# Mamba-2 chunk outputs: mask and log of dt inside the exponential, one product with C B for both directions

## The chip, the cores and the metric

One Trainium2 chip; the kernel runs on one of its cores. The metric is the device time of one execution in microseconds. The profile shows the core's engines: TensorE (PE, its weight loads apart as PEld), VectorE (DVE), ScalarE (ACT), GpSimd (POOL), and the queues that start DMA transfers (SP above all).

## The reference, cut to what matters

One layer of a hybrid trunk over 256 context and 1024 latent tokens, 1024 wide: a projection, three token mixers side by side (a Mamba-2 SSD, a gated unit, an S5 scan), a projection back and an MLP of 4096. The change lies in the SSD, which runs in both directions over chunks of 128 tokens, with 8 heads of 64 in two groups that share B and C. For one direction:

```python
a_cum = jnp.cumsum(dt * a.reshape(SSD_GROUPS, R), axis=2)
xdt = x * dt[..., None]
seg = a_cum[:, :, :, None] - a_cum[:, :, None, :]
lower = jnp.tril(jnp.ones((CHUNK, CHUNK), dtype=bool))[:, :, None, None]
lmat = jnp.exp(jnp.where(lower, seg, -jnp.inf))
cb = jnp.einsum('bcqgn,bckgn->bcqkg', cm, bm)
y_diag = jnp.einsum('bcqkg,bcqkgr,bckgrp->bcqgrp', cb, lmat, xdt)
...
y_off = jnp.einsum('bcqgn,bcgrpn,bcqgr->bcqgrp', cm, h_prev, jnp.exp(a_cum))
y = (y_diag + y_off).reshape(b_, L, H, P)
```

The mixer adds both directions and a skip term (`ssd_d` times x); `h_prev` is the state carried from chunk to chunk.

## The kernel before

There are 1280 tokens in 10 chunks (2 context, 8 latent) and two head groups g, so 20 chunks of outputs. `dt_chain` (L734 to L778) computes dt once for all chunks and both directions (`DTD`), the cumulative sums along the partitions (`col`: that of the forward direction, and the negative of the backward one), the factors for the states (`wdec`, `dtot`), and the same sums as rows, which it stores to DRAM (`rows_d`, L778).

`ssd_group` (L829) has two generators for a group. `right` (L869) runs the backward states over the chunks and keeps each as `hb`. `outputs` (L883) makes the outputs of one chunk a step:

- It loads the chunk's x, B and C (`xc`) and, by a DMA that gives every partition the same rows, `rb`: 2 directions x 4 heads x 128 sums (512 KB, three buffers).
- ScalarE takes exponentials of rb for the states' part (`er`, two halves of the partitions, L897).
- For each head ScalarE adds a column of `col` to rb's second half (L900) and VectorE subtracts the other column from the first half and takes the minimum (L901), which is the right one of the two differences on either side of the diagonal; one exponential over the four heads follows (L902).
- TensorE transposes x and B (`tok_major`, L842) and multiplies B by C into PSUM (`pcb`, L904). VectorE masks that product with the two triangles of `tri` into `cm` (L906).
- For each head ScalarE multiplies one triangle by dt (L910), and VectorE multiplies the other by its dt and adds (L911); VectorE multiplies all four heads by the exponentials (L912).
- TensorE multiplies the result by x into `py` (L918, eight parts of 64 rows in the trace) and the states by C into `po` (L925). VectorE scales `po` by er (L927), adds the skip term (L929, into cm again), GpSimd adds the two directions of er (L931), VectorE adds that (L932), and cm is stored (L933).
- `new_state` (L850) carries the forward state on: VectorE makes `xw`, TensorE multiplies it by B (L854), GpSimd decays the old state (L860), VectorE adds.

Each group's steps are handed to a scheduler together with other work: the slabs of the input projection whose columns these chunks need or that come behind (`xbc_slab`, `z_slab`), the S5 mixer's gate (`s5_glu`), `mixed_tile` and the first output projections (`out_slab`). The scheduler (`schedule_with_timeline_sim=True`, L1611) decides the order of the instructions on every engine. Helpers record most operations: L54 (`tt`, two tensors), L57 (`stt`, a tensor with a scalar column and a second tensor), L60 (`act`), L48 (`load`), so in the profile these are told apart by their tiles.

The tile that a chunk's masks and outputs share, and the order in which rb is used, in code:

```python
cm = pool.tile([128, 2, 128], F32, tag="cm", name="cm", bufs=2)
tt(cm, pcb.unsqueeze(1).to_broadcast([128, 2, 128]), tri[:, 0:2], ALU.mult)
...
    act(rb[:, 0, hh], cm[:, 0], ACT.Copy, scale=d0[:, hh:hh + 1])
    stt(rb[:, 0, hh], cm[:, 1], d1[:, hh:hh + 1], rb[:, 0, hh], ALU.mult, ALU.add)
tt(rb[:, 1], rb[:, 1], rb[:, 0], ALU.mult)
```

Of the kernel before, what the change touches and what calls it, by code (L numbers as in the profile page):

```python
# [10 lines left out]
F32 = mybir.dt.float32  # L11
F32R = mybir.dt.float32r
ACT = mybir.ActivationFunctionType
ALU = mybir.AluOpType
# [28 lines left out]
def trunk_kernel(ctx: ExitStack, tc: tile.TileContext, I, O):  # L43
# [690 lines left out]
    def dt_chain():  # L734
# [30 lines left out]
        for i, (m, d) in enumerate(((0, 0), (1, 1), (2, 0), (3, 1))):  # L765
            T.matmul(pc[:, i * 80:(i + 1) * 80], lhsT=tri[:, m, :], rhs=dta[:, d, :], start=True, stop=True)
        T.matmul(pc[:, 320:480], lhsT=ones, rhs=dta.rearrange("p d c -> p (d c)"), start=True, stop=True)
        S.copy(col[:, 0], pc[:, 0:80])
        act(col[:, 1], pc[:, 80:160], ACT.Copy, scale=-1.0)
        act(wdec.rearrange("p d c -> p (d c)"), pc[:, 160:320], ACT.Exp)  # L770
        tt(wdec, wdec, DTD, ALU.mult)
        act(dtot.rearrange("p d c -> p (d c)"), pc[:, 320:480], ACT.Exp)
# [53 lines left out]

    def ssd_group(pool, g):  # L829

        hb = {1: None}

# [35 lines left out]

        def right():  # L869
            px, bt, _ = tok_major(chunk_xbc(1, 3))  # L870
            hb[0] = new_state(f"hb{g}", 9, 1, 1, px, bt, None, "hb")
            yield
            px, bt, _ = tok_major(chunk_xbc(0, 3))
            hbf = new_state("hf", 2, 1, 0, px, bt, hb[0], "hbf")
            load(O["ssdo"][:, 512 + g * 256:512 + (g + 1) * 256], hbf)
            hb[9] = init(1, f"hb{g}", 9)
            yield
            for c in range(9, 2, -1):
                px, bt, _ = tok_major(chunk_xbc(c, 3))
                hb[c - 1] = new_state(f"hb{g}", 9, 1, c, px, bt, hb[c], "hb")  # L880
                yield

        def outputs():  # L883
            hf = None
            for c in range(NCH):
# [1 line left out]
                    load(O["ssdo"][:, g * 256:(g + 1) * 256], hf)  # L887
                    hf = init(0, "hf", 2)
                xc = chunk_xbc(c, 4)
                rb = pool.tile([128, 2, 4, 128], F32, tag="rb", name="rb", bufs=3)  # L890
                load(rb, rows_d[:, c * 8 + g * 4:c * 8 + g * 4 + 4, :].partition_broadcast(128))
                cf, cbk = scal(col, 0, c), scal(col, 1, c)

                er = pool.tile([128, 2, 2, 128], F32, tag="er", name="er", bufs=3)
                for par in range(2):
                    rs = slice(par * 64, (par + 1) * 64)
                    act(er[rs], rb[rs].rearrange("p d (a e) q -> p d a e q", e=2)[:, :, :, par], ACT.Exp)  # L897

                for hh in range(4):
                    act(rb[:, 1, hh], rb[:, 1, hh], ACT.Identity, bias=cbk[:, hh:hh + 1])  # L900
                    stt(rb[:, 1, hh], rb[:, 0, hh], cf[:, hh:hh + 1], rb[:, 1, hh], ALU.subtract, ALU.min)  # L901
                act(rb[:, 1], rb[:, 1], ACT.Exp)  # L902
                px, bt, pcb = tok_major(xc)
                T.matmul(pcb, lhsT=xc[:, 2], rhs=xc[:, 3], start=True, stop=True)  # L904
                cm = pool.tile([128, 2, 128], F32, tag="cm", name="cm", bufs=2)
                tt(cm, pcb.unsqueeze(1).to_broadcast([128, 2, 128]), tri[:, 0:2], ALU.mult)  # L906

                d0, d1 = scal(DTD, 0, c), scal(DTD, 1, c)
                for hh in range(4):
                    act(rb[:, 0, hh], cm[:, 0], ACT.Copy, scale=d0[:, hh:hh + 1])  # L910
                    stt(rb[:, 0, hh], cm[:, 1], d1[:, hh:hh + 1], rb[:, 0, hh], ALU.mult, ALU.add)  # L911
                tt(rb[:, 1], rb[:, 1], rb[:, 0], ALU.mult)  # L912
                xs = pool.tile([128, 4, 64], F32, tag="xs", name="xs", bufs=2)
                S.copy(xs, px)
                py = bank("wb", 2)[:, 0:256].rearrange("p (a q) -> p a q", a=2)
                for a in range(2):
                    for par in range(2):
                        T.matmul(py[par * 64:(par + 1) * 64, a, :], lhsT=xs[:, 2 * a + par], rhs=rb[:, 1, 2 * a + par],  # L918
                                 start=True, stop=True)
                hs_ = (hf, hb[c])  # L920
                dirs = [d for d in range(2) if hs_[d] is not None]
# [3 lines left out]
                        T.matmul(po[:, d, a], lhsT=hs_[d][:, a * 128:(a + 1) * 128], rhs=xc[:, 3], start=True, stop=True)  # L925
                ds = slice(dirs[0], dirs[-1] + 1)
                tt(er[:, ds], po[:, ds], er[:, ds], ALU.mult)  # L927
                for a in range(2):
                    stt(cm[:, a], xc[:, a], dcol[:, 2 * g + a:2 * g + a + 1], py[:, a], ALU.mult, ALU.add)  # L929
                if len(dirs) == 2:  # L930
# [143 lines left out]
    dt_chain()  # L1074
    psA.close()
    with tc.tile_pool(name="pd", bufs=1) as pd, banks("psB"):
        (right0, out0), (right1, out1) = [ssd_group(pd, g) for g in range(2)]
        def drain(g):
            for _ in g:
                pass  # L1080

        drain(right0)
        for m in (2, 3, 5, 7):
            xbc_slab(m)
        for c, _ in enumerate(out0):
            if c >= 5:
                next(right1, None)
                next(right1, None)
        drain(right1)
        for m in (0, 1):  # L1090
            z_slab(m, z_weights(m), (0, 1, 2))
        s5_glu()
        for c, _ in enumerate(out1):
            if c == 0:
                wz = [z_weights(m) for m in (2, 3)]
            if c in (0, 4):
                for m in (2, 3):
                    z_slab(m, wz[m - 2], (2,) if c else (0, 1))
            if c == 7:
                acc = [acc_tile(m) for m in range(4)]  # L1100
                wo = [out_weights(m) for m in range(2)]
                for m in range(2):
                    out_slab(m, (0,), wo[m])
            if c in (2, 6):
                mixed_tile(c // 4)
        stt(gs2, mod[:, 32:40, :], 1.0, g2.unsqueeze(2).to_broadcast([128, 8, 2]), ALU.add, ALU.mult)
        for m in range(2):
            out_slab(m, (1,), wo[m])
        for m in (2, 3):
            out_slab(m, (0, 1))  # L1110
# [504 lines left out]
```

## Time and profile before

| | |
|---|---|
| median of 3 runs | 1580.24 us (1580.15 to 1582.12) |
| the profiled execution's own time | 1578.67 us |
| its span, first to last instruction | 1576.7 us |
| TensorE busy | 1423.4 us (90%) |
| VectorE busy | 1067.9 us (68%) |
| ScalarE busy | 751.1 us (48%) |
| GpSimd busy | 389.5 us (25%) |
| mean granted TensorE clock | 0.947 of full speed |

Shares over the whole span mix stages: the output chunks fill some 200 us of it, the MLP most of the rest. What a change in one stage can do is read from that stage's windows and waits. A row of the lines view gives a group's line, engine, operation and tiles (out<-in), shapes and count, then its busy time in us, the mean of one in ns, and the engine's idle time just before with what ended it. In the timeline a row begins with the start and the duration in us; an xN at its end counts instructions merged into it.

### The profile page before, as it was taken

Reading aid. Unit: us, or ns where it says so; the run is one execution under the profiler, and the core shown is the slowest. Engines: PE = TensorE matmul, PEld = TensorE weight load, DVE = VectorE, ACT = ScalarE, POOL = GpSimd, SP = SyncE. Lnnn points to the kernel's source line nnn. Section 1 sums busy time; section 2 is a strip of 40 time slices with the busy share of each in tenths; the row PEclk is TensorE's granted clock in tenths of the full one; section 3 lists DMA queues with packets and bytes.
Section 4 is the critical chain, followed back from the end, with each engine's and each line's share of the span. In section 5 each row is a group of like instructions: output and inputs, shape, how many; then the busy total and the mean of one; then the engine's idle time right before and its main releaser. Section 6 shows DMA issues by size and latency. Waiting matters only on the chain.

```text
span 1576.7 us, 23817 instructions
## 1 busy us (share of the span) xinstructions
PE 1423.4 (90%) x8360; PEld 1202.6 (76%) x8360; DVE 1067.9 (68%) x1929; ACT 751.1 (48%) x1541; POOL 389.5 (25%) x487
## 2 busy tenths in 40 slices
PE   4689898999787779989999999999899999999795
PEld 3567676778565568878888888888788888887795
DVE  5773368668667885558977764674564768979945
ACT  3643434456645753437655554554555334424322
POOL 4555466613011122321100000000241313032033
PEclk9699999999997879999999999999999999999897
DMA  9759785264675647346444443344744245315312
GB/s 326 251 174 252 227 285 159 88 171 119 181 228 149 172 145 236 122 123 195 138 158 149 149 139 116 125 148 151 250 149 146 70 158 174 121 54 182 112 35 100
DMA packets 238903, 253.29 MB, mean 161 GB/s; under 512 B 15648, under 2 KB 163136, under 8 KB 238784
## 3 DMA queue, kind: packets, MB, share of 16 engines
q1 hardware_dynamic: 222880, 234.51, 48.2%
q10 hardware_dynamic: 15904, 17.27, 3.4%
q8 instruction: 66, 1.08, 0.3%
q14 instruction: 53, 0.43, 0.1%
HBM read 182.82 MB, written 68.89 MB: 160 GB/s over the span
## 4 chain that ended last, share of the span: by engine, by line
PE 58%; DVE 8%; DMA 6%; ACT 2%; issue 2%; POOL 1%; SPq 0%; DVEq 0%; ACTq 0%; POOLq 0%
PE ps_w L1215 7%; PE ps_w L1213 7%; PE ps_w L1214 7%; PE ps_w L1369 6%; PE ps_w L1370 6%; PE ps_w L1371 6%; PE ps_mm L219 4%; PE ps_mm L221 4%; PE ps_mm L220 4%; DMA rb<-rows_d 2%; PE ps_mm L1371 1%; PE ps_mm L1370 1%; PE ps_mm L1369 1%; DVE X L54 1%; DVE rb L57 1%
## 5 line engine op out<-in xcount | busy, mean ns | idle before, releaser
L219 PE MATMUL ps_mm<-hi,wh 128*128 128x512 f32 (+1 forms) x576 | 211.6, 367 | 20.1 <-DVE dtr L707 16.0
L221 PE MATMUL ps_mm<-hi,wl 128*128 128x512 f32 (+1 forms) x576 | 209.4, 364 | 0.9 <-DVE wl L54 0.9
L220 PE MATMUL ps_mm<-lo,wh 128*128 128x512 f32 (+1 forms) x576 | 209.8, 364 | 0.0
L1369 PE MATMUL ps_w<-uB,uA 128*128 128x512 f32 (+1 forms) x520 | 190.6, 371 | 9.3 <-ACT uB L60 8.9
L1370 PE MATMUL ps_w<-uB,uA 128*128 128x512 f32 (+1 forms) x520 | 191.3, 368 | 7.9 <-DVE uB L54 7.9
L1371 PE MATMUL ps_w<-uB,uA 128*128 128x512 f32 (+1 forms) x520 | 190.2, 367 | 0.0
L54 POOL TENSOR_TENSOR cb<-h 128x512 f32<-128x512 f32 x14 | 21.9, 1571 | 512.7 <-DMA h<-w 402.4
L219 PEld LDWEIGHTS ps_mm<-hi,wh 128*128 128x128 f32 x576 | 111.2, 193 | 38.1 <-DVE dtr L707 16.8
L221 PEld LDWEIGHTS ps_mm<-hi,wl 128*128 128x128 f32 x576 | 111.0, 193 | 18.1 <-DVE wl L54 1.8
L220 PEld LDWEIGHTS ps_mm<-lo,wh 128*128 128x128 f32 x576 | 111.0, 193 | 15.0 <-issue 0.6
L1369 PEld LDWEIGHTS ps_w<-uB,uA 128*128 128x128 f32 x520 | 99.9, 193 | 25.2 <-ACT uB L60 9.3
L1370 PEld LDWEIGHTS ps_w<-uB,uA 128*128 128x128 f32 x520 | 100.2, 193 | 24.7 <-DVE uB L54 9.8
L1371 PEld LDWEIGHTS ps_w<-uB,uA 128*128 128x128 f32 x520 | 99.8, 192 | 15.5
L60 ACT ACTIVATE uB<-tb 128x512 fp32r<-128x512 f32 x106 | 65.9, 625 | 64.9 <-PE ps_w L1371 31.7
L54 DVE TENSOR_TENSOR uB<-tb,uB 128x512 fp32r<-128x512 f32 x106 | 87.6, 846 | 13.1 <-ACT uB L60 13.1
L54 DVE TENSOR_TENSOR X<-X,ps_w 128x512 f32<-128x512 f32 x84 | 56.1, 680 | 27.7 <-PE ps_w L1371 27.6
L54 DVE TENSOR_TENSOR q<-q,ps_w 128x512 f32<-128x512 f32 x48 | 32.9, 685 | 59.7 <-PE ps_w L1215 59.0
L54 DVE TENSOR_TENSOR wl<-wraw,wh 128x1024 fp32r<-128x1024 f32 x32 | 48.4, 1514 | 36.7 <-ACT wh L60 35.9
L60 ACT ACTIVATE c<-c 128x512 f32<-128x512 f32 x64 | 40.3, 629 | 57.8 <-DVE c L54 56.9
L1371 PE MATMUL ps_mm<-ch,uA 128*128 128x256 f32 x224 | 63.2, 283 | 0.0
L1370 PE MATMUL ps_mm<-cl,uA 128*128 128x256 f32 x224 | 63.2, 283 | 0.0
L1369 PE MATMUL ps_mm<-ch,uA 128*128 128x256 f32 x224 | 63.1, 283 | 0.0
(435 smaller groups left out, 3875.3 us busy)
## 6 DMA issues: line engine op xcount, KB each, us to landing
rw<-w SPq DMA_DIRECT2D x112, 256.0 KB
tb<-a_d SPq DMA_DIRECT2D x106, 256.0 KB
aw<-ada_w SPq DMA_DIRECT2D x64, 256.0 KB
h<-w SPq DMA_DIRECT2D x32, 512.0 KB
a_d<-t SPq DMA_DIRECT2D x42, 256.0 KB
rb<-rows_d SPq DMA_DIRECT2D x20, 512.0 KB
adaw<-ada_w SPq DMA_DIRECT2D x32, 256.0 KB
wraw<-w_out SPq DMA_DIRECT2D x16, 512.0 KB
```

The source lines that it names most:

```text
L54: eng.tensor_tensor(out=out, in0=a, in1=b, op=op)
L57: V.scalar_tensor_tensor(out=out, in0=a, scalar=sc, in1=b, op0=op0, op1=op1)
L60: S.activation(out=out, in_=in_, func=func, **kw)
L219: T.matmul(out, lhsT=wh(k), rhs=xh(k), start=(k == 0), stop=False)
L220: T.matmul(out, lhsT=wh(k), rhs=xl(k), start=False, stop=False)
L221: T.matmul(out, lhsT=wl(k), rhs=xh(k), start=False, stop=(k == nk - 1))
L1213: T.matmul(out, lhsT=wh, rhs=X[0][:, j, :], start=(j == 0), stop=False)
L1214: T.matmul(out, lhsT=wh, rhs=X[1][:, j, :], start=False, stop=False)
L1215: T.matmul(out, lhsT=wl, rhs=X[0][:, j, :], start=False, stop=(j == 3))
L1369: T.matmul(out, lhsT=wh, rhs=bh, start=start, stop=False)
L1370: T.matmul(out, lhsT=wh, rhs=bl, start=False, stop=False)
L1371: T.matmul(out, lhsT=wl, rhs=bh, start=False, stop=stop)
```

## The change

`dt_chain` now fills `col` with log(dt) minus the cumulative sum, for both directions, with dt held above 1e-37. A constant tile `cap` is 0 where a direction's triangle holds and -1e30 elsewhere. In `outputs` GpSimd adds cap to each direction's rows into a tile of its own, `sg` (two buffers); ScalarE takes eight exponentials, one for each direction and head, with the column of col as bias, so that mask and dt are inside the exponential; VectorE adds the two directions and multiplies the sum by C B straight from PSUM. rb has two buffers in place of three, the output cm has a tile of its own with three, and the two groups share 16 buffers of backward states.

```diff
--- before.py
+++ after.py
@@ dt_chain
-        S.copy(col[:, 0], pc[:, 0:80])
-        act(col[:, 1], pc[:, 80:160], ACT.Copy, scale=-1.0)
+        V.tensor_scalar(out=col, in0=DTD, scalar1=1e-37, scalar2=None, op0=ALU.max)
+        act(col, col, ACT.Ln)
+        fl = col.rearrange("p d c -> p (d c)")
+        tt(fl, fl, pc[:, 0:160], ALU.subtract)
...
@@ ssd_group
-            hb[0] = new_state(f"hb{g}", 9, 1, 1, px, bt, None, "hb")
+            hb[0] = new_state("hb", 16, 1, 1, px, bt, None, "hb")
...
-                rb = pool.tile([128, 2, 4, 128], F32, tag="rb", name="rb", bufs=3)
+                rb = pool.tile([128, 2, 4, 128], F32, tag="rb", name="rb", bufs=2)
                 load(rb, rows_d[:, c * 8 + g * 4:c * 8 + g * 4 + 4, :].partition_broadcast(128))
-                cf, cbk = scal(col, 0, c), scal(col, 1, c)
+                sg = pool.tile([128, 2, 4, 128], F32, tag="sg", name="sg", bufs=2)
+                for d in range(2):
+                    tt(sg[:, d], rb[:, d], cap[:, d].unsqueeze(1).to_broadcast([128, 4, 128]), ALU.add, G)
...
-                for hh in range(4):
-                    act(rb[:, 1, hh], rb[:, 1, hh], ACT.Identity, bias=cbk[:, hh:hh + 1])
-                    stt(rb[:, 1, hh], rb[:, 0, hh], cf[:, hh:hh + 1], rb[:, 1, hh], ALU.subtract, ALU.min)
-                act(rb[:, 1], rb[:, 1], ACT.Exp)
+                for d in range(2):
+                    cd = scal(col, d, c)
+                    for hh in range(4):
+                        act(sg[:, d, hh], sg[:, d, hh], ACT.Exp, bias=cd[:, hh:hh + 1])
+                tt(sg[:, 0], sg[:, 0], sg[:, 1], ALU.add)
                 px, bt, pcb = tok_major(xc)
                 T.matmul(pcb, lhsT=xc[:, 2], rhs=xc[:, 3], start=True, stop=True)
-                cm = pool.tile([128, 2, 128], F32, tag="cm", name="cm", bufs=2)
-                tt(cm, pcb.unsqueeze(1).to_broadcast([128, 2, 128]), tri[:, 0:2], ALU.mult)
-
-                d0, d1 = scal(DTD, 0, c), scal(DTD, 1, c)
-                for hh in range(4):
-                    act(rb[:, 0, hh], cm[:, 0], ACT.Copy, scale=d0[:, hh:hh + 1])
-                    stt(rb[:, 0, hh], cm[:, 1], d1[:, hh:hh + 1], rb[:, 0, hh], ALU.mult, ALU.add)
-                tt(rb[:, 1], rb[:, 1], rb[:, 0], ALU.mult)
+                tt(sg[:, 0], pcb.unsqueeze(1).to_broadcast([128, 4, 128]), sg[:, 0], ALU.mult)
...
+                cm = pool.tile([128, 2, 128], F32, tag="cm", name="cm", bufs=3)
...
+        cap = pd.tile([128, 2, 128], F32, name="cap")
+        V.tensor_scalar(out=cap, in0=tri[:, 0:2], scalar1=-1.0, scalar2=1e30, op0=ALU.add, op1=ALU.mult)
```

The instructions' order on VectorE, second group, before: rb_5203, rb_5262 and rb_5396 are the tiles of chunks 1, 2 and 3; cm, er, xw and hf are as named above.

```order
L54 TENSOR_TENSOR xw_5250<-ps_wa_5217,wdec_131 128x256
L54 TENSOR_TENSOR rb_5203<-rb_5203 128x512
L54 TENSOR_TENSOR hf_5254<-hf_5254,ps_ws_5252 128x256
L54 TENSOR_TENSOR cm_5283<-ps_wa_5276,pk2_90 128x256
L57 SCALAR_TENSOR_TENSOR rb_5396<-rb_5396,col_130 128x128 x3
L57 SCALAR_TENSOR_TENSOR cm_5224<-xc_5201,pk2_90,ps_wb_5237 128x128 x2
L57 SCALAR_TENSOR_TENSOR rb_5396<-rb_5396,col_130 128x128
L57 SCALAR_TENSOR_TENSOR rb_5262<-cm_5283,DTD_129,rb_5262 128x128
L54 TENSOR_TENSOR er_5205<-ps_wb_5242,er_5205 128x256
L57 SCALAR_TENSOR_TENSOR rb_5262<-cm_5283,DTD_129,rb_5262 128x128 x3
L54 TENSOR_TENSOR xw_5312<-ps_wa_5276,wdec_131 128x256
L54 TENSOR_TENSOR cm_5224<-cm_5224,er_5205 128x256
```

Between the products xw of two chunks stand the masks of one chunk and the differences of the next but one, ten instructions in all.

The same engine and place in the change: sg_5323 and sg_5376 are the tiles of chunks 3 and 4, cm_5231 and er_5198 belong to chunk 2; y is the gating of `mixed_tile`.

```order
L57 SCALAR_TENSOR_TENSOR cm_5231<-xc_5191,pk2_90,ps_wb_5220 128x128 x2
L54 TENSOR_TENSOR sg_5323<-sg_5323 128x512
L54 TENSOR_TENSOR er_5198<-ps_wb_5225,er_5198 128x512
L54 TENSOR_TENSOR sg_5323<-ps_wa_5338,sg_5323 128x512
L54 TENSOR_TENSOR hf_5241<-hf_5241,ps_ws_5239 128x256
L54 TENSOR_TENSOR xw_5365<-ps_wa_5338,wdec_131 128x256
L54 TENSOR_TENSOR cm_5231<-cm_5231,er_5198 128x256
L57 SCALAR_TENSOR_TENSOR y_5260<-z_5261,y_5260 128x256
L57 SCALAR_TENSOR_TENSOR cm_5359<-xc_5319,pk2_90,ps_wb_5348 128x128 x2
L54 TENSOR_TENSOR sg_5376<-sg_5376 128x512
```

The sum and the product of a chunk now stand on either side of the chunk before's er, with nothing of a later chunk ahead of them.

VectorE in the change at the end of the first group: sg_4498 and sg_4581 are the tiles of chunks 7 and 8, cm_4451 the output of chunk 6, hb a backward state of the second group, ze the gate's projection.

```order
L54 TENSOR_TENSOR cm_4451<-cm_4451,er_4418 128x256
L54 TENSOR_TENSOR sg_4581<-sg_4581 128x512
L54 TENSOR_TENSOR hb_4476<-hb_4476,ps_ws_4474 128x256
L57 SCALAR_TENSOR_TENSOR ze_5076<-ze_5076,ps_mm_5051 128x512
L54 TENSOR_TENSOR sg_4498<-ps_wa_4513,sg_4498 128x512
```

Here the sum of chunk 8 stands ahead of the product of chunk 7; chunk 8's sg is the buffer that chunk 6 used.

GpSimd at that place before (tiles of chunks 6 and 7 of the first group and of the second group's backward states):

```order
L54 TENSOR_TENSOR hbf_4438<-hb_4424,dtot_132 128x256
L54 TENSOR_TENSOR hb_4515<-h0_4442,dtot_132 128x256
L54 TENSOR_TENSOR hf_4500<-hf_4409,dtot_132 128x256
L54 TENSOR_TENSOR hf_4589<-hf_4500,dtot_132 128x256
L54 TENSOR_TENSOR er_4448<-er_4448 128x256
L54 TENSOR_TENSOR hb_4530<-hb_4515,dtot_132 128x256
```

and in the change, where er_4418 is chunk 6's and sg_4581 chunk 8's:

```order
L54 TENSOR_TENSOR hbf_4405<-hb_4391,dtot_132 128x256
L54 TENSOR_TENSOR hb_4476<-h0_4409,dtot_132 128x256
L54 TENSOR_TENSOR hf_4461<-hf_4376,dtot_132 128x256
L54 TENSOR_TENSOR sg_4581<-rb_4579,cap_3534 128x512 x2
L54 TENSOR_TENSOR er_4418<-er_4418 128x256
L54 TENSOR_TENSOR hf_4544<-hf_4461,dtot_132 128x256
```

The two sums of chunk 8 stand ahead of chunk 6's er and of the state's decay.

## Rows read from the trace of the kernel before

**Rows 1.** Windows: us, busy time (count) of PE, PEld, DVE, ACT, POOL; clock, DMA share, GB/s.

```profile
400.00:580.00 180.00, 134.78 (x685) 104.23 (x684) 130.94 (x345) 112.53 (x283) 31.61 (x43) 0.81 0.65 176
580.00:620.00 40.00, 40.00 (x237) 34.77 (x236) 20.44 (x34) 11.56 (x18) 10.09 (x9) 1.00 0.75 243
483.00:512.00 29.00, 20.34 (x103) 14.35 (x103) 21.80 (x64) 17.97 (x53) 3.57 (x6) 0.74 0.62 153
```

**Rows 2.** Tile rb: ns min/median/max, first and last start in us, forms.

```profile
L918 PE MATMUL ps_wb<-rb,xs x160: 272/323/476, 389.7 to 589.5; 128*64 128x128 f32 x160
...
L54 DVE TENSOR_TENSOR rb<-rb x20: 673/682/1511, 386.2 to 576.2; 128x512 f32<-128x512 f32 x20
```

**Rows 3.** Waits from 325 to 620 us: total in us, times, longest.

```profile
ACT er L60 <- DMA rb<-rows_d: 28.8, 10, 5.3
PE ps_ws L854 <- DVE xw L54: 23.4, 8, 4.7
...
DVE rb L57 <- ACT rb L60: 21.1, 9, 5.4
```

**Rows 4.** Timeline from 482 to 513 us: one rb buffer, and three chunks' matmuls.

```profile
484.57 0.36 SPq L48 DMA_DIRECT2D rb<-rows_d  x1
...
490.29 0.63 ACT L60 ACTIVATE er<-rb 64x512 f32<-64x512 f32 x1
...
491.82 0.66 PE L918 MATMUL ps_wb<-rb,xs 128*64 128x128 f32 x8 [0.21 <-DVE rb L54]
...
503.44 0.67 DVE L54 TENSOR_TENSOR rb<-rb 128x512 f32<-128x512 f32 x1
...
504.82 1.12 PE L918 MATMUL ps_wb<-rb,xs 128*64 128x128 f32 x8
...
511.61 1.12 PE L918 MATMUL ps_wb<-rb,xs 128*64 128x128 f32 x8
```

**Rows 5.** Lines of VectorE, 320 to 600 us: the operations that go.

```profile
L57 DVE SCALAR_TENSOR_TENSOR rb<-rb,col 128x128 f32<-128x128 f32 x80 | 27.2, 380 | 17.0 <-ACT rb L60 17.0
L57 DVE SCALAR_TENSOR_TENSOR rb<-cm,DTD,rb 128x128 f32<-128x128 f32 x80 | 25.9, 369 | 4.2 <-ACT rb L60 4.2
...
L54 DVE TENSOR_TENSOR rb<-rb 128x512 f32<-128x512 f32 x20 | 15.4, 772 | 0.0
...
L54 DVE TENSOR_TENSOR cm<-ps_wa,pk 128x256 f32<-128x256 f32 x20 | 8.4, 420 | 9.3 <-DMA y_d<-cm 8.9 <-PE ps_wa L904 0.4
```

**Rows 6.** Lines of ScalarE, 240 to 760 us: the operations that go.

```profile
L60 ACT ACTIVATE rb<-rb,col 128x128 f32<-128x128 f32 x80 | 26.3, 391 | 0.5
L60 ACT ACTIVATE rb<-cm,DTD 128x128 f32<-128x128 f32 x80 | 25.4, 390 | 4.5 <-DVE cm L54 4.4
...
L60 ACT ACTIVATE rb<-rb 128x512 f32<-128x512 f32 x20 | 12.5, 629 | 4.1 <-DVE rb L57 4.0
```

**Rows 7.** Timeline of ScalarE at 403 us: a table load and what follows it.

```profile
403.26 1.28 ACT L60 ACT_TABLE_LOAD   x1 [1.00 <-DMA yf<-y_d]
404.56 1.28 ACT L60 ACTIVATE yf<-yf 128x1288 f32<-128x1288 f32 x1
```

**Rows 8.** Timeline from 517 to 520 us: VectorE with GpSimd beside it.

```profile
516.55 0.68 DVE L54 TENSOR_TENSOR er<-ps_wb,er 128x512 f32<-128x512 f32 x1
...
517.58 0.90 POOL L54 TENSOR_TENSOR er<-er 128x256 f32<-128x256 f32 x1
...
517.82 1.21 DVE L54 TENSOR_TENSOR rb<-rb 128x512 f32<-128x512 f32 x1
...
518.49 1.12 POOL L54 TENSOR_TENSOR sq<-sq,z 128x256 f32<-128x256 f32 x1
```

**Rows 9.** GpSimd: tile sq at 555 us; the page's group; its lines from 320 us.

```profile
L54 POOL TENSOR_TENSOR sq<-sq,z x3: 1265/1266/1271, 555.8 to 565.7; 128x512 f32<-128x512 f32 x3
...
L54 POOL TENSOR_TENSOR cb<-h 128x512 f32<-128x512 f32 x14 | 21.9, 1571 | 512.7 <-DMA h<-w 402.4
...
L54 POOL TENSOR_TENSOR er<-er 128x256 f32<-128x256 f32 x16 | 12.4, 774 | 50.9 <-DVE er L54 41.5 <-ACT rb L60 9.4
```

More of the change, by code (lines that the diff above doesn't have):

```diff
@@ L825, in xbc_slab, with ssd_group @@
         load(xbc_d[g, a], acc)
-    def ssd_group(pool, g):
+    def ssd_group(pool, g, cap):
         hb = {1: None}
@@ L875, in right @@
             load(O["ssdo"][:, 512 + g * 256:512 + (g + 1) * 256], hbf)
-            hb[9] = init(1, f"hb{g}", 9)
+            hb[9] = init(1, "hb", 16)
             yield
@@ L879, in right @@
                 px, bt, _ = tok_major(chunk_xbc(c, 3))
-                hb[c - 1] = new_state(f"hb{g}", 9, 1, c, px, bt, hb[c], "hb")
+                hb[c - 1] = new_state("hb", 16, 1, c, px, bt, hb[c], "hb")
                 yield
@@ L917, in outputs @@
                     for par in range(2):
-                        T.matmul(py[par * 64:(par + 1) * 64, a, :], lhsT=xs[:, 2 * a + par], rhs=rb[:, 1, 2 * a + par],
+                        T.matmul(py[par * 64:(par + 1) * 64, a, :], lhsT=xs[:, 2 * a + par], rhs=sg[:, 0, 2 * a + par],
                                  start=True, stop=True)
@@ L1076, in trunk_kernel @@
     with tc.tile_pool(name="pd", bufs=1) as pd, banks("psB"):
-        (right0, out0), (right1, out1) = [ssd_group(pd, g) for g in range(2)]
+        cap = pd.tile([128, 2, 128], F32, name="cap")
+        V.tensor_scalar(out=cap, in0=tri[:, 0:2], scalar1=-1.0, scalar2=1e30, op0=ALU.add, op1=ALU.mult)
+        (right0, out0), (right1, out1) = [ssd_group(pd, g, cap) for g in range(2)]
         def drain(g):
```

## The prediction

> **What bounds the kernel now.** I read the windows first [rows 1]. From 400 to 580 us TensorE works only 134.78 of 180 us, at a granted clock of 0.81 of full speed; from 580 on it works all of 40 us at 1.00. So the time to be won lies before 580, and behind it the program is bound by TensorE. In 400 to 580 VectorE is busy 130.94 us, ScalarE 112.53, GpSimd 31.61: no engine is full, and VectorE comes nearest to TensorE. The matmuls of y (L918) run from 389.7 to 589.5 us [rows 2]: 20 chunks in 200 us, so this stretch is the output chunks' own.
>
> The list of waits says what TensorE stands still for there: 23.4 us for xw, a short VectorE product that stands in VectorE's queue behind the work on rb [rows 3]. VectorE in turn waits 21.1 us for ScalarE in the middle of that work (two engines alternating over four heads), and ScalarE 28.8 us for the landing of rb. The timeline of three chunks shows the loop [rows 4]: the matmul of y starts at 491.82 and at 511.61 three chunks later, 6.6 us a chunk. One rb buffer is refilled at 484.57, is first read at 490.29 (5.7 us later), is multiplied at 503.44 and used at 504.82. It is held for about 20 us, and three buffers of 20 us give 6.7 us a chunk, which is the measured interval. So where few projections stand between chunks, the life of rb sets the pace, and the queues of VectorE and ScalarE make that life long.
>
> **The change, part by part.**
>
> VectorE [rows 5]. Removed, for 20 chunks: the subtract and min, 27.2 us; the two masks, 25.9; the product, 15.4; the masking of CB, 8.4: 76.9 us. Added per chunk: one sum of the two directions, 128x512 from SBUF, as the product that goes (772 ns), and one product with CB from PSUM, as er with po, whose 512-wide form took 0.68 us [rows 8]. That is 20 x 1.45 = 29 us. Net -48 us, or -2.4 us a chunk. The one-off work on col and cap is four short instructions ahead of the chunks, beside projections; I count nothing for it, and if it weren't covered it would cost about 1 us.
>
> ScalarE [rows 6]. Removed: 26.3 + 25.4 + 12.5 = 64.2 us. Added: 160 exponentials of 128x128 with a column as bias, the form of the Identity that goes (80 took 26.3 us): 52.6 us. Two more table loads of 1.28 us stand in the new order, since square roots now fall between exponentials: +2.6 us. Net -9 us. The log itself comes while the table of the other log is loaded and brings no load.
>
> After the load at 403.26 the next activation starts at 404.56, so a load costs its 1.28 us here and hardly more [rows 7]. The Trainium skill (ScalarE: Activation LUTs, "What ACT_TABLE_LOAD costs") adds a drain and puts a switch at about 2.66 us; the two would be 5.3 us by that, and the sum 2.7 us higher. The rows don't show such a drain.
>
> GpSimd [rows 9]. Added: 40 sums of 128x512. The nearest rows: 1.27 us (same width, two SBUF operands, in this stretch) and 1.57 us (in a busier stretch). I take 1.27, since it was measured here: 51 us more, 2.5 us a chunk. With the er sum (0.77) and a state product (under 1) that is some 4 us of a chunk's 6.6, so GpSimd isn't the bound by load.
>
> What the sums do to VectorE: at 517.82 the product of two SBUF tensors took 1.21 us with GpSimd working beside it, while er with po, one operand in PSUM, took 0.68 at 516.55 [rows 8]; the product's undisturbed median is 0.68 [rows 2]. So about half of the overlapped time is lost by operations that read two SBUF tensors. The change leaves one large such operation a chunk in this work in place of nine. If half of the 51 us met such an operation, VectorE would lose 13 us of the 48; it is then still 35 us lighter, so I put nothing on the path.
> The Trainium skill (GPSIMD Engine Reference, "Key points") states the same contention, for DVE instructions with two SBUF inputs. Taken at its worst it would stretch VectorE under all 51 us, by 25 us, half of what the change frees; the sum would then lose about half of its second term below, 4 us.
>
> Buffers and queues. rb is now free once er and the two sums have read it, 5.7 us of landing plus 2.5 of sums and some queueing after its load; two buffers of 9 us allow 4.5 us a chunk. SP's queue, in which the loads of xc and z stand behind the rb load, is held less. The sg buffer lives from the sums to the matmul of y: 2.5 (sums) + 1.3 (the second four exponentials) + 0.77 + 0.68 + 1.1 (matmuls), 6.4 us; two of them allow 3.2 us a chunk. In the new order VectorE's xw stands behind one sum and one product, not behind some nine operations. The new wait is GpSimd's for a free sg: behind it stand the er sum and the state's product; for the er sum waits VectorE's cm.
>
> **The sum**, against the profiled execution (span 1576.7, its own time 1578.67).
> 1. Intervals with few projections: 12 of the 19 in the new order. In 483 to 512 us TensorE works 20.34 of 29 us [rows 1], so at that clock it alone needs 4.6 us of 6.6; ScalarE and GpSimd need about 4. I take 5.5, near the middle between 4.6 and 6.6: 12 x -1.1 = -13.2 us (bounds -24 and 0).
> 2. The other intervals, filled with projections: of the 23.4 us of waits for xw some lie in term 1; I take -8 (bounds -16 and 0).
> 3. Clock: a mean of 0.81 between the two levels (1.2 and 2.4 GHz) means 38% of 180 us at the lower one, 68 us; with TensorE busy for three quarters of it, half of 51 us, 26 us, went to the slower clock. It comes back where idling ends; with a fifth of the idle time gone I take -4 (bounds -13 and 0).
> 4. Table loads on ScalarE: +2.6.
> Together -22.6: a span of 1554.1, a time of 1556.1. The median of the runs is 1.6 us above the profiled execution, so **1558 us**.
>
> **The rivals.**
> A, more: TensorE becomes the bound of the dense intervals. 12 x -2 = -24, xw -16, clock -10, loads +2.6: -47, 1533 us. For it: no other engine is above 4.5 us a chunk. Against: in-order queues have left a quarter of VectorE's time unused so far.
> B, nothing: the chunks keep their pace, because the landing of rb (5.7 us), the state's recurrence and the projections set it; what is freed becomes idle time. 1577 to 1582 us. For it: ScalarE's largest wait is for a landing [rows 3], and there are two rb buffers now, not three. That the change doesn't do what it says belongs here too: the instruction order shows the operations gone, so only their wait could stay.
> C, slower: GpSimd in series. In part of the new order (chunks 6 to 9 of the first group) VectorE's sum for chunk c+2 stands ahead of its product for chunk c+1. That sum needs GpSimd's sums into a buffer which the matmul of chunk c frees. Then the 6.4 us above are one chunk's, not two chunks'. It decides from the point where two GpSimd sums exceed 6.6 - 3.9 = 2.7 us, 1.35 each; at 1.57, and 0.5 us of queueing on ScalarE, a chunk takes 7.5 us: 12 x 0.9 + 2.6 = +13, 1594 us. For it: 1.57 was measured in another stretch. Against: only those few chunks stand so, and most of them are filled with projections anyway.
> The Trainium skill (GPSIMD Engine Reference, "Engine selection") speaks for C: it advises VectorE for elementwise work on two inputs, as GpSimd is about twice as slow. The rows agree (1.27 against 0.68), and by that rule alone the change moves work the wrong way.
>
> **How the numbers follow.** Forecast (a gain of 10 to 34 us) 0.58; A 0.16; B 0.15; C 0.11. A measurement of this kernel can tell about 0.2%, 3 us, from no change. B splits: 0.06 on the faster side, 0.08 within, 0.01 slower. Faster 0.80, same 0.08, slower 0.12. The range reaches to 1532, where A lies, and to 1582, the end of B; outside remain about 0.07 below and 0.11 above.
>
> **What would show it.** In the profile after: VectorE's busy time about 45 us lower, ScalarE's 5 to 10 lower, GpSimd's 50 to 60 higher; y matmuls at 5 to 6 us where they stand alone; the wait for xw below 12 us; the last y matmul about 20 us earlier; a granted clock above 0.81 in the stretch. Wrong would be: sums above 1.4 us; a large wait of ScalarE for GpSimd on sg, or of VectorE for the er sum; intervals still at 6.6 us with a lighter VectorE (B).

## The result and the profile after

The changed kernel takes 1560.59 us in the median of four runs (1552.92 to 1562.64), the kernel before 1581.18 (1580.15 to 1582.43): a ratio of 0.9861, 95% interval 0.9825 to 0.9896. Timed again in five rounds it gave 0.9858 (0.9842 to 0.9874), so the gain is some 22 us, 1.4%. The profiled execution is the fastest of its four (1552.92 us, span 1551.1); a second profile (a0_after, span 1558.1) is read beside it.

Busy time by engine, from the page of the change:

```profile
PE 1409.7 (91%) x8360; PEld 1190.7 (77%) x8360; DVE 1042.4 (67%) x1772; ACT 737.8 (48%) x1518; POOL 449.6 (29%) x527
```

Against the table of before: VectorE 25.5 us lower, ScalarE 13.3, GpSimd 60.1 higher, and TensorE 13.7 lower although its instructions are as many (x8360).

Windows of the changed kernel in the stretches of [rows 1] (us, then busy time and count of PE, PEld, DVE, ACT, POOL; clock, DMA share, GB/s):

```profile
400.00:580.00 180.00, 143.86 (x810) 114.70 (x811) 119.09 (x228) 106.58 (x272) 84.20 (x81) 0.91 0.72 210
580.00:620.00 40.00, 38.94 (x233) 34.34 (x232) 20.70 (x30) 11.82 (x20) 4.49 (x4) 1.00 0.43 134
```

TensorE works 9 us more of the 180, at 0.91 in place of 0.81, and finishes 810 matmuls there in place of 685. Since the work in a fixed window differs, I compare the whole stage, from the first transpose of the chunks to the last projection's matmul, which holds the same matmuls in both. Before:

```profile
324.40:697.50 373.10, 320.98 (x1688) 261.74 (x1686) 256.65 (x524) 204.03 (x437) 86.09 (x87) 0.91 0.57 164
```

The change, first profile:

```profile
321.80:673.40 351.60, 308.48 (x1691) 252.29 (x1690) 228.07 (x364) 190.72 (x415) 144.66 (x127) 0.95 0.60 175
```

and second:

```profile
325.00:677.20 352.20, 313.50 (x1691) 255.66 (x1690) 228.25 (x364) 190.61 (x415) 145.46 (x127) 0.94 0.60 175
```

The stage is 21.5 and 20.9 us shorter; what lies behind it is the same to 2 us, and in the first profile the part ahead of it is 2.6 us shorter too. Of that, TensorE's idle time (length less PE) fell from 52.1 to 43.1 and 38.7 us, and its time for the same matmuls from 321.0 to 308.5 and 313.5. So between a third and more than half of the gain is shorter time for matmuls that were there before. The granted clock of the stage rose with it, from 0.91 to 0.95 and 0.94, so I read this part as the clock.

Where the time went shows when the stage is cut at the matmuls of y: first to eighth (among the projections), eighth to twentieth (few projections), and behind the twentieth. The change, first profile:

```profile
383.10:453.30 70.20, 64.16 (x378) 50.69 (x378) 46.47 (x86) 48.15 (x113) 35.68 (x31) 1.00 0.79 228
453.30:543.70 90.40, 64.85 (x362) 50.34 (x361) 63.56 (x126) 58.73 (x162) 50.82 (x49) 0.81 0.62 173
543.70:673.40 129.70, 120.47 (x640) 102.24 (x640) 75.63 (x112) 49.79 (x81) 35.46 (x26) 1.00 0.46 148
```

The kernel before took 83.6 and 116.2 us for the first two (its rows stand under e5_before_rb4), and for the third:

```profile
589.50:697.50 108.00, 105.47 (x555) 89.41 (x551) 61.38 (x90) 41.82 (x68) 31.71 (x24) 1.00 0.47 152
```

The chunks end 46 us earlier, but 75 of the projections' matmuls now stand behind them, and the part behind them is 21.7 us longer. TensorE's idle time went from 15.0 to 6.0 us among the projections, from 31.8 to 25.6 where few stand, and from 2.5 to 9.2 behind the chunks (in a0_after to 5.5, 24.2 and 6.7).

Waits in the change, 325 to 620 us, that answer to [rows 3] or are new (total in us, times, longest):

```profile
POOL sg L54 <- PE ps_wb L918: 17.6, 8, 6.4
ACT sg L60 <- POOL sg L54: 16.0, 7, 5.0
PE ps_wb L918 <- ACT xs L914: 11.1, 8, 3.2
PE ps_wa L911 <- ACT bt L850: 10.5, 8, 2.8
ACT xs L914 <- DVE sg L54: 9.2, 7, 2.6
ACT er L60 <- DMA rb<-rows_d: 5.8, 1, 5.8
PE ps_ws L857 <- DVE xw L54: 2.6, 2, 1.7
```

The waits for xw (23.4 us) and ScalarE's for the landing of rb (28.8) are all but gone; GpSimd waits for a landing once, 10.7 us ahead of the first chunk. In their place TensorE waits for ScalarE's copies of x and B, which stand in ScalarE's queue among the exponentials, and ScalarE waits for GpSimd and, with the copy xs, for VectorE's product. The timeline of the change shows the new loop (start and duration in us; xN counts merged instructions):

```profile
477.42 0.66 PE L918 MATMUL ps_wb<-sg,xs 128*64 128x128 f32 x8 [1.07 <-ACT xs L914]
478.17 2.96 POOL L54 TENSOR_TENSOR sg<-rb,cap 128x512 f32<-128x512 f32 x2 [1.25 <-PE ps_wb L918]
480.30 1.28 ACT L60 ACTIVATE sg<-sg,col 128x128 f32<-128x128 f32 x4
481.74 1.27 ACT L60 ACTIVATE sg<-sg,col 128x128 f32<-128x128 f32 x4
481.88 0.66 PE L918 MATMUL ps_wb<-sg,xs 128*64 128x128 f32 x8 [1.07 <-ACT xs L914]
483.12 1.40 DVE L54 TENSOR_TENSOR sg<-sg 128x512 f32<-128x512 f32 x1
485.10 0.68 DVE L54 TENSOR_TENSOR sg<-ps_wa,sg 128x512 f32<-128x512 f32 x1
485.99 0.35 ACT L914 COPY xs<-ps_wa 128x256 f32<-128x256 f32 x1
486.39 0.66 PE L918 MATMUL ps_wb<-sg,xs 128*64 128x128 f32 x8 [1.39 <-ACT xs L914]
```

The matmul of y at 477.42 frees an sg; GpSimd's two sums start at 478.17, the exponentials follow, VectorE's sum and product, the copy xs, and at 486.39 the matmul of the chunk after next. One sg is held for 9.0 us, two of them give 4.5 us a chunk; in [rows 4] it was 6.6. Two things limit this reading. These are adjoining intervals, 4.9, 4.5 and 4.5 us; over all twelve from the eighth matmul of y to the twentieth the mean fell from 9.7 to 7.5 us. And sg's life need not be what sets the 4.5 us. Windows of the two intervals, 4.46 and 4.51 us long:

```profile
477.42:481.88 4.46, 2.55 (x19) 1.85 (x19) 4.01 (x9) 4.40 (x14) 3.71 (x3) 1.00 0.71 190
481.88:486.39 4.51, 2.55 (x19) 1.85 (x19) 3.94 (x9) 4.45 (x14) 2.96 (x3) 1.00 0.63 190
```

ScalarE is busy 4.40 and 4.45 us of them: its own work fills the loop, and sg may be held only as long as that takes. No run with three whole sg buffers tells the two apart.

### The profile page after: what moved, and what is told of

Same layout as the page of the kernel before. It is cut to its first block, busy times and chain, and to the rows that moved or that the text cites. A ratio compares the mean times of both kernels' runs of the same rounds, so it can differ in the third digit from the quotient of the medians.

```text
span 1551.1 us, 23671 instructions
## 1 busy us (share of the span) xinstructions
PE 1409.7 (91%) x8360; PEld 1190.7 (77%) x8360; DVE 1042.4 (67%) x1772; ACT 737.8 (48%) x1518; POOL 449.6 (29%) x527
## 4 chain that ended last, share of the span: by engine, by line
PE 54%; DVE 9%; DMA 6%; ACT 4%; issue 2%; POOL 1%; SPq 0%; DVEq 0%; ACTq 0%; POOLq 0%
PE ps_w L1218 7%; PE ps_w L1216 7%; PE ps_w L1217 7%; PE ps_w L1372 6%; PE ps_w L1373 6%; PE ps_w L1374 6%; PE ps_mm L221 3%; PE ps_mm L219 3%; PE ps_mm L220 3%; DMA z<-z_d 2%; DVE X L54 2%; PE ps_mm L1373 1%; PE ps_mm L1374 1%; PE ps_mm L1372 1%; DVE uA L54 1%
## 5 line engine op out<-in xcount | busy, mean ns | idle before, releaser
L219 PEld LDWEIGHTS ps_mm<-hi,wh 128*128 128x128 f32 x576 | 110.1, 191 | 39.4 <-DVE dtr L707 13.6
L1372 PEld LDWEIGHTS ps_w<-uB,uA 128*128 128x128 f32 x520 | 99.8, 193 | 25.6 <-ACT uB L60 9.8
L54 POOL TENSOR_TENSOR sg<-rb,cap 128x512 f32<-128x512 f32 x40 | 55.5, 1410 | 42.7 <-PE ps_wb L918 17.6
L60 ACT ACTIVATE c<-c 128x512 f32<-128x512 f32 x64 | 40.3, 629 | 56.4 <-DVE c L54 55.5
L1374 PE MATMUL ps_mm<-ch,uA 128*128 128x256 f32 x224 | 63.2, 283 | 0.0
```

Of the source, the lines that this page charges most:

```text
L54: eng.tensor_tensor(out=out, in0=a, in1=b, op=op)
L60: S.activation(out=out, in_=in_, func=func, **kw)
L219: T.matmul(out, lhsT=wh(k), rhs=xh(k), start=(k == 0), stop=False)
L1372: T.matmul(out, lhsT=wh, rhs=bh, start=start, stop=False)
L1374: T.matmul(out, lhsT=wl, rhs=bh, start=False, stop=stop)
```

## The experiments

All were timed in five rounds beside the kernel before, whose median was 1581.5 to 1581.7 us in the three sets. The table gives for each the stage as read above from one window row of its profile: length, TensorE's work, and the rest, idle time.

| kernel | median us | ratio to before (95%) | stage | work | idle | clock |
|---|---|---|---|---|---|---|
| before | 1581.5 | 1 | 373.1 | 321.0 | 52.1 | 0.91 |
| a0_after | 1559.01 | 0.9858 (0.9842-0.9874) | 352.2 | 313.5 | 38.7 | 0.94 |
| e1_sums_vector | 1563.76 | 0.9887 (0.9872-0.9903) | 356.9 | 315.0 | 41.9 | 0.93 |
| e2_sums_twice | 1586.57 | 1.0031 (1.0019-1.0044) | 376.0 | 320.0 | 56.0 | 0.91 |
| e3_split31 | 1565.37 | 0.9902 (0.9886-0.9918) | 360.4 | 314.2 | 46.2 | 0.93 |
| e4_rb3 | 1557.17 | 0.9842 (0.9825-0.9860) | 352.1 | 310.3 | 41.8 | 0.94 |
| e5_before_rb4 | 1571.61 | 0.9933 (0.9917-0.9950) | 361.6 | 312.8 | 48.8 | 0.93 |
| e6_before_gw | 1583.02 | 1.0007 (0.9991-1.0023) | 378.2 | 322.9 | 55.3 | 0.90 |
| e7_inplace | 1568.59 | 0.9916 (0.9900-0.9933) | 365.7 | 315.7 | 50.0 | 0.92 |
| e8_before_buffers | 1571.64 | 0.9933 (0.9919-0.9948) | 366.0 | 318.1 | 47.9 | 0.91 |
| e9_rb3_sg2 | 1559.04 | 0.9855 (0.9837-0.9874) | 351.0 | 309.2 | 41.8 | 0.95 |
| e10_filler | 1571.19 | 0.9932 (0.9919-0.9944) | 361.4 | 321.3 | 40.1 | 0.97 |
| e11_rb3_one_each | 1567.82 | 0.9903 (0.9886-0.9921) | 359.7 | 314.7 | 45.0 | 0.92 |

The profiled executions of e3, e6 and e11 (1570.1, 1588.9 and 1569.8 us) are 5, 6 and 2 us slower than their kernels' medians, so their stage rows are long by about as much.

The scheduler orders every variant anew. By the traces TensorE's order stays closest to that of its parent in e5 and e9; in the others the projections are dealt out differently, most of all in e7, and a few us of their differences may come from that.

**a0_after**: the change, unedited.

> The changed kernel once more, for a second trace and a tighter ratio. Median 1557 to 1562 us (ratio 0.985 to 0.988). In the trace the first profile's reading should come back: from the first state matmul at 321 us to the last projection the stretch took 377 us before and 353 in the first profile of the change, of which TensorE stood idle 52.6 and 43.7, and worked 324.4 and 309.3 for the same matmuls. If the clock gives most of the gain, a slower execution shows a lower granted clock and longer busy time at about the same idle time; if idling gives it, the idle time moves instead.

The gain came back. This execution is slower than the first profile by longer work (313.5 against 308.5) with less idle time, so what the clock gives varies between executions.

**e1_sums_vector**:

```diff
-tt(sg[:, d], rb[:, d], cap[:, d]..., ALU.add, G)
+tt(sg[:, d], rb[:, d], cap[:, d]..., ALU.add)
```

> The 40 mask sums on VectorE, all else as in the change. Theory of the prediction (a light VectorE queue is what pays): VectorE gets 40 x 0.68 = 27 us back, less some 10 us of stretching by GpSimd that goes; the gain over the kernel before shrinks to a third or a half: 1566 to 1574 us. Rival (elementwise work is misplaced on GpSimd, its 1.28 to 1.41 us stand in the chain from rb to the matmul of y, where VectorE would take 0.68): 1545 to 1557 us, with ScalarE's 16 us of waits for the sums gone. Third: VectorE has room for both, within 3 us of the change.

4.7 us slower than the change, between the first and the third expectation; the two intervals just overlap. So GpSimd is the better place in this program, by little. The 4.7 us are a net figure: VectorE took on 27.5 us of sums, and its busy time in the stage rose by 13.6 us (228.3 to 241.8), but each sum became shorter, and so did VectorE's sum of the two directions (1.05 to 0.71 us). The Trainium skill (GPSIMD Engine Reference, "Engine selection") would have these sums on VectorE; one takes 0.69 us there and 1.28 on GpSimd (medians), as it says, but the time does not follow the duration of one instruction here.

**e2_sums_twice**:

```diff
+tt(sg[:, d], sg[:, d], cap[:, d]..., ALU.add, G)
```

> Each mask sum made twice on GpSimd (adding the mask a second time leaves the exponentials 0 or unchanged), 40 more sums of 1.28 us. If GpSimd's sums lie beside other work with room to spare (prediction): GpSimd then has about 5.1 + 1.4 = 6.5 us a chunk against intervals of 5.5, so 12 x 1 = 12 us, up to 25 with queueing: 1570 to 1585 us. Rival C (the sums in series with ScalarE and VectorE): each added us counts in full, 40 x 1.28 = 51 us: 1600 to 1612 us. If even doubled they are hidden: within 4 us of the change.

27.6 us slower than the change, for 40 sums that took 56.5 us on GpSimd (201.1 against 144.7 us in the stage): half of each added us shows. Waits of this kernel, 325 to 620 us:

```profile
PE ps_wb L919 <- ACT xs L915: 26.8, 11, 5.2
DVE sg L54 <- ACT sg L60: 20.5, 13, 2.9
```

The chain of the loop above grows, and TensorE's wait for xs with it, from 11.1 to 26.8 us. The time lies 1.6 us above the first expectation's range and far below rival C's. So the sums have little slack, but do not count in full. The slope is not that of GpSimd's chain alone, since VectorE's busy time in the stage grew too, by 10.4 us (228.3 to 238.7).

**e3_split31** (three buffers for the half that is multiplied, one for the half that is added):

```diff
-sg = pool.tile([128, 2, 4, 128], F32, tag="sg", name="sg", bufs=2)
+sg = [pool.tile([128, 4, 128], F32, tag=f"sg{d}", name=f"sg{d}", bufs=3 if d == 0 else 1) for d in range(2)]
...
```

> The change with the two halves of sg as buffers of their own: three for the half that the matmul of y reads, one for the half that is only added to it, in the same room. In the profile of the change GpSimd waited 17.6 us for the matmuls of y to free sg, and ScalarE 16.0 us for GpSimd's sums. If those waits stand on the path: 4 to 9 us faster than the change, 1550 to 1556 us. If they are cover (another queue is late anyway, as in the kernel before, where a fourth rb buffer ended ScalarE's waits and left the dense intervals at 7 us): within 3 us of the change, 1556 to 1563.

6 us slower than the change: both expectations missed. GpSimd's waits in this kernel:

```profile
POOL sg L54 <- DMA rb<-rows_d: 31.8, 8, 10.8
POOL sg L54 <- DVE sg L54: 14.1, 8, 3.4
```

With a single buffer for the second half GpSimd waits for VectorE's sum; rb is held meanwhile, and the next landing comes late. Part of the 6 us may lie elsewhere: TensorE's one wait for the gate weights gw is 7.0 us here and 3.3 in the change.

**e4_rb3** (sg split in two and one buffers, three rb) and **e9_rb3_sg2** (sg as in the change, three rb):

```diff
-rb = pool.tile([128, 2, 4, 128], F32, tag="rb", name="rb", bufs=2)
+rb = pool.tile([128, 2, 4, 128], F32, tag="rb", name="rb", bufs=3)
...
```

> The change with three rb buffers (room from one buffer for the half of sg that is only added, and 14 state buffers for 16). If the landing of rb still holds chunks with two buffers (GpSimd waited 10.7 us for it once, ScalarE 5.8): 4 to 10 us faster than the change, 1549 to 1556 us. If rb is no longer the pace: within 3 us of it, 1556 to 1563.

> The change with a third rb buffer and sg as it is (12 state buffers for 16 make the room); the order of TensorE's work is nearly that of the change. If the landing of rb still sets the pace in places (with sg's second half in one buffer, three rb buffers gave 1557 and two 1565): 1549 to 1556 us, GpSimd's wait for rb's landing gone but for the first. If two are enough once sg is not the brake: within 3 us of the change, 1556 to 1562.

Both are level with the change within their intervals. Two rb buffers are enough once nothing else holds them; no version here is shown to beat the change.

**e5_before_rb4**:

```diff
-rb = pool.tile([128, 2, 4, 128], F32, tag="rb", name="rb", bufs=3)
+rb = pool.tile([128, 2, 4, 128], F32, tag="rb", name="rb", bufs=4)
```

> The kernel before with four rb buffers in place of three, nothing else. If the life of rb sets the pace where few projections stand (prediction: three of 20 us give 6.6 us a chunk), four give about 5 us, or the next bound at 5.5: 12 x 1.1 = 13 us less, 1562 to 1572 us, and ScalarE's wait for the landing of rb (28.8 us) falls below 10. Rival: the queues of VectorE and ScalarE set the pace and rb is only held as long as they take; a fourth buffer is then filled earlier and waits longer: 1577 to 1582 us.

10 us faster, with TensorE's order nearly unchanged, and ScalarE's wait for rb down from 28.8 to 5.0 us. In its place ScalarE waits for VectorE, 0.4 us before and now:

```profile
ACT er L60 <- DVE cm L54: 20.2, 12, 6.7
```

The gain is not where the prediction had it. Windows from the first matmul of y to the eighth, and from there to the twentieth. Before:

```profile
389.70:473.30 83.60, 68.62 (x374) 52.77 (x373) 55.41 (x142) 49.03 (x117) 13.60 (x17) 0.92 0.72 202
473.30:589.50 116.20, 84.43 (x436) 66.90 (x435) 91.58 (x233) 73.76 (x184) 22.35 (x29) 0.76 0.59 156
```

With four buffers:

```profile
391.80:464.70 72.90, 64.29 (x372) 50.26 (x371) 54.73 (x142) 49.06 (x117) 13.54 (x17) 0.97 0.78 231
464.70:579.50 114.80, 80.61 (x437) 63.64 (x435) 91.55 (x233) 74.45 (x184) 24.74 (x30) 0.80 0.60 154
```

All but 1.4 us come in the first stretch, among the projections: 6.4 us less idle and 4.3 us less work there, the clock up from 0.92 to 0.97. In the stretch with few projections the loop keeps its pace; this kernel's timeline there, three chunks apart:

```profile
488.75 1.12 PE L918 MATMUL ps_wb<-rb,xs 128*64 128x128 f32 x8
...
508.78 1.12 PE L918 MATMUL ps_wb<-rb,xs 128*64 128x128 f32 x8
```

20.03 us for three, 6.7 each, as before. So rb's life was an effect of the queues in that loop, not its cause.

**e6_before_gw**:

```diff
-gw = ev("gw").rearrange("p (k m) -> p k m", k=2)
-load(gw, I["gluw"].rearrange("(k p) m -> p k m", p=128), nc.scalar)
...
+gw = pd.tile([128, 2, 256], F32, name="gw")
+load(gw, I["gluw"].rearrange("(k p) m -> p k m", p=128))
```

> The kernel before with the gate weights gw loaded into a buffer of their own at the start of the chunk stage, by SP, in place of ScalarE's queue in the middle of it. In the profile before, that load was issued at 419.15, right behind ScalarE's wait for rb (er started at 417.83 after 4.9 us), TensorE waited 5.7 us for it, and its granted clock fell to 0.66 for the next 10 us; with a fourth rb buffer the wait was 1.2 us and the clock stayed at 1.00. If the 10 us that the fourth rb buffer brought came by this one place: 1571 to 1576 us (5.7 us of waiting and about 3 of clock, less what moves elsewhere). If they came from rb in general, this brings nothing: 1579 to 1583.

No gain: TensorE waits no more for gw, and the stage's idle time is 55.3 us all the same. The one wait of 5.7 us is not what the fourth rb buffer cured. (The order of the projections shifted too, so it is no proof that the wait was free.)

**e7_inplace**:

```diff
-rb = pool.tile([128, 2, 4, 128], F32, tag="rb", name="rb", bufs=2)
+rb = pool.tile([128, 2, 4, 128], F32, tag="rb", name="rb", bufs=3)
...
-sg = pool.tile([128, 2, 4, 128], F32, tag="sg", name="sg", bufs=2)
...
+sg = rb
```

with the two exponentials of er ahead of the sums.

> The change without sg: GpSimd adds the mask in place in rb, after ScalarE's exponentials of rb for er, and there are three rb buffers again; all arithmetic as in the change. rb is then held from its landing to the matmul of y, as before. If the arithmetic (a light VectorE queue) brings the gain: within 4 us of the change, 1556 to 1564. If the own buffers bring half of it, as the fourth rb buffer's 10 of 22 us suggest: 1566 to 1575, and ScalarE's or GpSimd's waits for the landing of rb come back above 20 us.

Without sg's own buffers 9.6 us of the gain are lost. Waits of this kernel:

```profile
POOL rb L54 <- ACT er L60: 40.4, 14, 6.5
ACT er L60 <- DMA rb<-rows_d: 23.0, 8, 5.7
```

The wait for rb's landing is back, as the second theory said. But the buffers are not all that differs: the sums now have to come behind er's exponentials (GpSimd's 40.4 us), TensorE's order is far from the change's, and its one wait for gw is 7.7 us in place of 3.3. The 9.6 us are the price of all this together.

**e8_before_buffers** (in the kernel before: cm of the outputs apart, three buffers; 16 shared state buffers):

```diff
-hb[c - 1] = new_state(f"hb{g}", 9, 1, c, px, bt, hb[c], "hb")
+hb[c - 1] = new_state("hb", 16, 1, c, px, bt, hb[c], "hb")
...
+cm = pool.tile([128, 2, 128], F32, tag="cy", name="cm", bufs=3)
```

> The kernel before with the change's other buffers alone: cm for the output in three buffers of its own, apart from the masked CB, and one pool of 16 state buffers for both groups; rb and all arithmetic as before. In the profile before VectorE waited 8.9 us for the stores of cm. If buffers in general hold the kernel before: 4 to 9 us faster, 1573 to 1578 us. If it is rb alone among the buffers (the fourth rb buffer brought 10 us, outputs put back in place in rb cost 10): within 3 us of before, 1578 to 1585.

10 us faster, against the second expectation and 1.4 us beyond the first. But TensorE's order differs widely from that of before (75 projection matmuls move behind the last chunk, as they do in the change), so buffers and order are not told apart here.

**e10_filler**:

```diff
+for _ in range(3 if g or c > 7 else 0):
+    T.matmul(wb[:, 256:512], lhsT=xc[:, 2], rhs=xc[:, 0:2]..., start=True, stop=True)
...
```

> The change with three more matmuls of 128x256 ahead of the matmuls of y in the 12 chunks that have few projections (the last two of the first group, all ten of the second); their result is not used. They cost TensorE 12 x 3 x 0.38 = 13.7 us at the full clock and twice that at the lower one. In the stretch with few projections TensorE works 57 of 80 us at a granted clock of 0.79. If the clock follows TensorE's idling and is worth what the profiles suggest: granted clock there above 0.9 and at least 5 us of the cost given back, 1556 to 1564 us. If the clock doesn't follow it: the cost less what fits in idle time, 1566 to 1575 us, clock near 0.79.

12 us slower, in the second expectation's range, but with the clock of the first. Windows of the stretch with few projections, ninth to last chunk, in a0_after:

```profile
466.00:546.00 80.00, 57.38 (x313) 44.66 (x315) 57.62 (x114) 53.50 (x147) 46.45 (x44) 0.79 0.63 180
```

and with the added matmuls:

```profile
471.00:557.00 86.00, 64.99 (x378) 50.52 (x378) 57.95 (x116) 54.37 (x146) 46.40 (x44) 0.92 0.59 155
```

The added group in this kernel's lines of TensorE:

```profile
L917 PE MATMUL ps_wb<-xc 128*128 128x256 f32 x72 | 19.7, 411 | 10.0 <-DVE er L54 9.8
```

72 parts took 19.7 us; without them the stage's work is 301.6 us, 7 to 12 below the change's. So activity does bring the clock back. But idle time stayed at 40.1 us: the added matmuls themselves waited 9.8 us for a bank that VectorE frees, so they stood behind a wait and not inside one.

**e11_rb3_one_each** (e9 with the first of a chunk's sums on VectorE):

```diff
-tt(sg[:, d], rb[:, d], cap[:, d]..., ALU.add, G)
+tt(sg[:, d], rb[:, d], cap[:, d]..., ALU.add, G if d else V)
```

> As the change with three rb buffers and 12 state buffers, and of the two mask sums of a chunk the first on VectorE, the second on GpSimd. If the two sums in series on GpSimd (2.6 us) are the longer way for a chunk now: 3 to 6 us faster than the same with both on GpSimd. If VectorE's queue is the dearer place (all 40 sums there cost 5 us): 2 to 4 us slower than it.

8.8 us slower than e9, in the direction of the second expectation, at more than twice its size. Waits of this kernel:

```profile
POOL sg L54 <- PE ps_wb L918: 28.1, 8, 7.8
ACT sg L60 <- DVE sg L54: 16.6, 6, 6.9
```

ScalarE now waits for the sum that stands in VectorE's queue. Why one sum there costs more than both (e1) stays open.

## Why the prediction was right, and where its steps were not

The time came out 2.6 us above the 1558 forecast, and the direction and size stand. By its steps:

- **Costs of the engines.** GpSimd: 1.27 us a sum was forecast. The median is 1.28, but the mean is 1.41, and the 40 sums took 55.5 us, not 51. So two of the signs that were named as wrong did come: sums above 1.4 us on average, and 16.0 us of ScalarE's waits for GpSimd on sg. The changed kernel's GpSimd and VectorE lines, 325 to 620 us:

```profile
L54 POOL TENSOR_TENSOR sg<-rb,cap 128x512 f32<-128x512 f32 x40 | 55.5, 1410 | 42.7 <-PE ps_wb L918 17.6 <-DMA rb<-rows_d 10.7 <-ACT ze L60 5.8
```

```profile
L54 DVE TENSOR_TENSOR sg<-sg 128x512 f32<-128x512 f32 x20 | 21.0, 1048 | 15.2 <-ACT sg L60 9.7 <-ACT bt L850 5.4
L54 DVE TENSOR_TENSOR sg<-ps_wa,sg 128x512 f32<-128x512 f32 x20 | 13.6, 682 | 0.4 <-PE ps_wa L911 0.3
```

  In place of 29 us VectorE's new work takes 34.6. Its busy time in the stage fell by 28.6 us (256.7 to 228.1), where 45 was named as the sign: beside the dearer sum, operations that stayed took some 8 us longer (the gating y of 128x512 went from 713 to 1037 ns), and some 6 us of the removed durations had overlapped with their neighbours', which a sum of durations counts twice. ScalarE fell by 13.3 us, more than the 5 to 10 named.
- **Term 4, two more table loads (+2.6 us): wrong sign.** It was read from the order of instructions, not from a trace. Over the whole program, before and after:

```profile
L60 ACT ACT_TABLE_LOAD x20 | 25.7, 1283 | 8.1 <-issue 2.4 <-DMA rb<-rows_d 2.3 <-DMA mix_d<-vq 1.7
```

```profile
L60 ACT ACT_TABLE_LOAD x18 | 23.1, 1283 | 5.4 <-issue 2.4 <-DMA mix_d<-vq 1.5 <-DMA yf<-y_d 1.3
```

  Two loads fewer, -2.6 us. The swing of 5.2 us covers the 4.3 us by which ScalarE's fall went beyond the 9 forecast.
- **Term 1, the dense intervals (-13.2): half of it, and not by the cause named.** The adjoining intervals went further than the 5.5 us forecast, to 4.5 (477.42 to 486.39 is two chunks, 9.0 us). But 6.6 us was the pace of a few intervals and was multiplied by 12; twelve took 9.7 us on average before. TensorE's idle time from the eighth matmul of y to the twentieth fell by 6.2 us (7.6 in a0_after). The stated cause fell: "the life of rb sets the pace", 3 buffers of 20 us. Four buffers left 6.7 us (e5). That the loop needed fewer steps between engines is my reading of the order; no run shows it by itself. A further rb buffer pays in the other stretch, among the projections, which the prediction left out. The life of sg was forecast at 6.4 us and measured 9.0; whether it is a bound or again an effect, with ScalarE's queue full, is open.
- **Term 2, the waits for xw (-8).** They fell by 20.8 us (23.4 to 2.6), but new waits for xs and bt of TensorE took most of that back: 21.6 us against 6.9 before. TensorE's idle time among the projections fell by 9.0 us (9.5 in a0_after), near the term. What no term had is the stretch behind the chunks, where idle time rose by 6.7 us (4.2), and the projections that moved there: the last matmul of y came 46 us earlier, not 20. Terms 1 and 2 together forecast 21 us less idle time; 9.0 and 13.4 were measured.
- **Term 3, the clock (-4): mis-sized.** The same matmuls took 12.5 and 7.5 us less. The terms' sum came out right by luck: this error and those of the other terms cancelled.
- **What carries the gain.** This stays open in part. With the outputs' own buffers but without sg's (e7) 13 of the 22 us remain, of which e8 has 10 without the new arithmetic; sg's own buffers, with the order that they allow, go with 9.6. What VectorE's lighter queue is worth alone was not measured: 27 us of sums put back cost 4.7 (e1), net of what their shorter durations gave. So the prediction named the right place. That it gave too much to VectorE's load and too little to how long a buffer waits is likely, but not shown. How the arithmetic, the buffers and TensorE's order share the gain can't be told, since a fourth rb buffer alone also gives 10 and the parts don't add.
- **Rivals.** B (nothing) and A (-47) did not come. C's chain is there, as the loop shows, and e2 shows a slope of half a us for each. C's price was even passed: the mean sum of 1.41 us lies above its 1.35, and two sums took 2.96 us in the loop, above its 2.7. It did not decide because two chunks share the loop's 9.0 us. In the place that C named, between the matmuls of y of chunks 7, 8 and 9 of the first group, nothing was won: 8.8 and 10.4 us, against 10.1 and 8.5 before.

## What to carry to other kernels

A buffer that is held long may be the cause of a pace or its effect; one more buffer, with the instruction order nearly unchanged, tells which, and where. Before you blame its life, look at how busy each engine is over one turn of the loop. Where TensorE idles at a lowered clock, count every us of idle time that goes as more than one, by what your own profiles show. And price an operation moved to a second engine by the chain that it joins: doubling it shows the slack.

## What was not expected of the hardware

**Idle time carries work with it.** Over the 13 profiles of the table without the filler (the change's two included), the stage's work and idle time lie near one line: each us less idle goes with 0.66 us less time for the same matmuls (correlation 0.81). The granted clock moves between 0.90 and 0.95 alike. This is a relation over versions; that TensorE's activity moves the clock is shown by e10_filler alone.

**GpSimd beside VectorE.** VectorE's sum of two SBUF tensors took 1048 ns on average beside GpSimd's sums (1.40 us in the loop above, right under a pair of them), and 708 ns where those sums are on VectorE itself, in e1:

```profile
L54 DVE TENSOR_TENSOR sg<-sg 128x512 f32<-128x512 f32 x20 | 14.2, 708 | 9.5 <-ACT sg L60 9.4
L54 DVE TENSOR_TENSOR sg<-ps_wa,sg 128x512 f32<-128x512 f32 x20 | 13.7, 683 | 3.2 <-PE ps_wa L911 3.0
```

The product with one operand in PSUM kept its 682 ns. The Trainium skill (GPSIMD Engine Reference, "Key points") names this contention for two SBUF inputs; the trace agrees, and prices it here at 20 x 0.34 = 6.8 us.
